# Output products by chunk with eight accumulating banks, half of the one-hots on ACT, and look-ups in half precision on DVE

## The chip, the core and the metric

The kernel runs on one core of a Trainium2 chip. The metric is the device time of one execution in microseconds (us), the median over runs. The core's engines work side by side, each through its own instructions in order: PE (matrix products; PEld is its weight load), DVE (vector), ACT (scalar functions, copies), POOL (general), SP (issues DMAs). They wait for each other by semaphores. PE writes into PSUM, eight banks of 128 x 512 f32 values; DVE and ACT empty them into SBUF.

## The reference

The model is a stack of blocks over 512 tokens of width 1024: a mixer of attentions, a mixture of experts (PEER), a gated projection, then two further blocks with their feed-forward parts. All is f32. The change lies in the PEER part alone:

```
s1, s2 = scores of the query's halves against 128 keys each
v1, i1 = top_k(s1, 16);  v2, i2 = top_k(s2, 16)
cand = v1[..., :, None] + v2[..., None, :]
sc, pos = top_k(cand, 16)
eidx = take_along_axis(i1 * 128 + i2, pos);  g = softmax(sc)
a = einsum('thkd,td->thk', expert_u[eidx], h)
out = einsum('thk,thkd->td', gelu(a) * g, expert_v[eidx])
```

There are 8 heads, 16 picks a head, so 128 picks a token, and 16384 experts.

## The kernel before

It computes PEER in two ways. For the first 128 tokens (`SP`) it fetches the picked rows by indirect DMA, 128 rows of u and then 128 of v for all tokens at once, and multiplies them on DVE (L1022, L1026; a "gather" below). For the other 384 (`ND`) it computes all experts: `up` takes the 128 chunks of 128 experts in turn, PE multiplies chunk and tokens, ACT applies Gelu out of the bank (L1088) and writes it to the DRAM array `ad`. Meanwhile a dense matrix G of weights is built in the DRAM array `Gd`: for each token the one-hots of i1 and i2 (L960, L961), the second one multiplied by the weight's upper and lower part (L964, r1 and r2), and a product of 128x128 per token and part on PE (L939), evacuated by ACT (L941) and written every 24 tokens (L945). In the down half, `ad` and G come back, DVE multiplies them (L1081), ACT rounds the product to its upper part (L113) and DVE takes the lower part (L1068).

Every f32 product with weights is three matmuls: upper weights by upper activations (L198), upper by lower (L199), lower by upper (L200). A unit of weights, 128 x 1024, is loaded by SP (L89) into one of four raw buffers, split by ACT into wh (four buffers) and by DVE into wl (L107, three buffers). `take` hands out unit i after it has issued wl of unit i+2, wh of i+3 and the load of i+6.

The down half before: 16 groups of eight chunks. `prepare(g + 1)` makes all of a group's activations while group g runs; PE begins a group when all eight are issued. For each of eight output blocks it makes 24 matmuls into one of two mm banks, and DVE adds the bank to x (L1122).

Side work is issued by generators. After every 12 counted matmuls `tick` steps them: `fetched` (gathers, one every `pace` ticks, in the down half spread over 228 ticks), `routing` (`select`, which picks experts for 128 tokens with the look-ups at L898, L901 and L905, and `build_g`, eight tokens a step), `prepare`, `load_g`. A chunk of 24 matmuls has two ticks, after its 6th matmul (tick A) and its 18th (tick B). A step of `build_g` takes 3 or 4 ticks by turns; its products (`g_products`) are issued one tick after r1 and r2, in two halves of four tokens.

In up the banks are the two mm banks; the products use s, the transposes pt.

Of the kernel before, what the change touches and what calls it, by code (L numbers as in the profile page):

```python
# [15 lines left out]
OP = mybir.AluOpType  # L16
# [17 lines left out]


class Net:
    def __init__(self, tc, ctx, a, units):
# [17 lines left out]
        self.width = T  # L55
# [691 lines left out]
    def peer(self, ctx):  # L747
# [8 lines left out]
        u_ctx = ExitStack()  # L756
        self.slots = u_ctx.enter_context(self.tc.tile_pool(name="slot2", bufs=19))
# [4 lines left out]
        io16, iota2 = fixed("io16", 16), fixed("iota2", 256, F16)  # L762
# [79 lines left out]
        def select(i):  # L842


            fi = slot("If")
# [40 lines left out]
            nc.vector.tensor_tensor(r[0], r[0], r[2], OP.add)  # L886
            nc.vector.tensor_tensor(r[1], r[1], r[3], OP.add)
# [5 lines left out]
            for half in range(2):  # L893
                tab = fi[:, half * 128:(half + 1) * 128].rearrange("p (h a) -> p h a", h=8)
                for hp in range(4):
                    e = slot("eq")
                    e3 = e.rearrange("p (s a) -> p s a", a=16)
                    nc.vector.tensor_tensor(e3, io16[:, None, :].to_broadcast([128, 32, 16]),  # L898
                                            r[half][:, hp * 32:hp * 32 + 32, None].to_broadcast([128, 32, 16]), OP.is_equal)
                    e4 = e.rearrange("p (h s a) -> p h s a", h=2, s=16)  # L900
                    nc.gpsimd.tensor_tensor(e4, e4, tab[:, 2 * hp:2 * hp + 2, None, :].to_broadcast([128, 2, 16, 16]), OP.mult)  # L901
# [24 lines left out]
            sel[i] = o  # L926
# [22 lines left out]
        def build_g(i):  # L949
            o = sel.pop(i)  # L950
            it = iota2.rearrange("p (i t) -> p i t", t=2)[:, None].to_broadcast([128, 4, 128, 2])
            for t in range(0, 128, 8):
# [10 lines left out]
                for j, r in enumerate((r1, r2)):  # L963
                    nc.vector.tensor_tensor(r, o2, col(2 + j), OP.mult)  # L964
# [3 lines left out]
        self.pace = 3  # L968

        def routing():  # L970
# [5 lines left out]
            for i in range(1, 4):  # L976
                nxt = select(i + 1) if i < 3 else None
                for n, w in enumerate(build_g(i)):
# [3 lines left out]
                    if i == 2 and nxt is None:  # L982
                        self.pace = 2
# [4 lines left out]
            self.pace = 1  # L988
            yield from load_g(0)
            yield 2  # L990
            self.spawn(prepare(0))
            yield from load_g(1)

        gather = {"tile": lambda: self.hp.tile([128, D], F32, tag="a", name=self.nm("row"))}
# [8 lines left out]
        def fetched():  # L1003
# [4 lines left out]
            def fetch(n):  # L1008
                if n < len(jobs):
                    m, k = jobs[n]  # L1010
                    rows[n] = gather["tile"]()
# [4 lines left out]
            for n, (m, k) in enumerate(jobs):  # L1016
                if self.pace is None and not left:
                    left.append(spread(len(jobs) - n, 228))
                yield next(left[0], 1) if left else self.pace
# [12 lines left out]
            for b in range(2):  # L1032
                yield 1
                pt = self.psum("pt")
                for j in range(4):
                    c = 4 * b + j
                    nc.tensor.transpose(pt[:, j * 128:(j + 1) * 128], y_tok[:, c * 128:(c + 1) * 128], self.ident)
                for j in range(4):
                    x = self.x[4 * b + j][:, 0:SP]
                    nc.vector.tensor_tensor(x, pt[:, j * 128:(j + 1) * 128], x, OP.add)  # L1040
            y_done.append(1)

        C, G, ready = {}, {}, {g: 0 for g in range(16)}
# [7 lines left out]
        def prepare(g):  # L1051

            if g:
                C[g] = [parts(self.act_tile()) for _ in range(8)]
            else:
                C[g] = [tuple(v[:, 0:ND] for v in p) for p in pairs(8, "C")]
            gt = G.pop(g)
            src = {}

            def fetch(k):  # L1060
                if k < 8:
                    src[k] = (self.hp.tile([128, D], F32, tag="a", name=self.nm("ar")) if g < 2 and k % 2 else self.slot("ar"))[:, 0:ND]
                    nc.sync.dma_start(src[k], ad[g * 8 + k])

            def split(k, a):
                self.round_hi(C[g][k][0], a)
                yield 1
                nc.vector.tensor_tensor(C[g][k][1], a, C[g][k][0].bitcast(F32), OP.subtract)  # L1068
                ready[g] += 1

            def split_later(k, a):
                yield 2
                yield from split(k, a)
            fetch(0)
            fetch(1)
            for k in range(8):
                fetch(k + 2)
                yield 1 + k % 2
                a = src.pop(k)
                v = a.rearrange("p (b t) -> p b t", t=TB)  # L1080
                nc.vector.tensor_tensor(v, v, gt[:, :, k * TB:(k + 1) * TB], OP.mult)  # L1081
                self.spawn(split_later(k, a))
# [11 lines left out]

        def up(c):
            self.width = ND
            self.linear(hh, 1, lambda _, ps: gelu(c, ps))
            self.width = T
# [9 lines left out]
        self.width = ND  # L1108
        self.pace = None
        for g in range(16):  # L1110
            last = g == 15
            until(lambda: ready[g] == 8)
            if g == 1:
                u_ctx.close()
                self.slots = ctx.enter_context(self.tc.tile_pool(name="slot3", bufs=7))
                rows = ctx.enter_context(self.tc.tile_pool(name="rows3", bufs=6))
                wide = lambda dt=F32: rows.tile([128, D], dt, tag="row", name=self.nm("row"))
                gather["tile"] = wide

            def evac(c, ps):  # L1120
                x = self.x[c][:, SP:]
                nc.vector.tensor_tensor(x, ps, x, OP.add)  # L1122
                if last:
                    if c == 0:
                        self.norm_begin(self.gains[:, 16:24])
                    self.norm_chunk(c)
            if not last:
                self.spawn(prepare(g + 1))
                if g < 14:
                    self.spawn(load_g(g + 2))  # L1130
            else:
                until(lambda: y_done)
                pp = []
                for k in range(2):
                    p = h_tok[:, k * 512:(k + 1) * 512]
                    nc.scalar.dma_start(p, self.a["p"][k])
                    t = wide(F32R)
                    pp.append((t[:, 0:512], t[:, 512:1024]))
                    self.hilo(p, *pp[k])
            for c in range(8):  # L1140
                self.linear_one(C[g], c, evac)
            C.pop(g)
        self.width = T
        t = [y_tok, h_tok, wide(), wide()]
        self.ple(pp, [v[:, k * 512:(k + 1) * 512] for v in t for k in range(2)])

    def linear_one(self, act, c, evac):
        self.linear(act, 1, lambda _, ps: evac(c, ps))
# [534 lines left out]
def host(i):  # L1683
# [44 lines left out]
    v = i["peer_expert_v"][0].reshape(128, 16, 8, 8, 128)  # L1728
    o["peer_v"] = v.transpose(1, 3, 0, 2, 4).reshape(128, 128, 1024)
# [66 lines left out]
```

## Time and profile before

| | us |
|---|---|
| median of 3 runs (2986.84 to 2990.61) | 2987.37 |
| the profiled execution | 2987.24 |
| its span, first to last instruction | 2985.5 |
| PE busy | 2877.2 (96%) |
| DVE busy | 1997.2 (67%) |
| ACT busy | 1255.2 (42%) |
| POOL busy | 558.8 (19%) |

The profile is of one execution. Busy PE time includes the pipelining of matmuls, so that two of them overlap in it. The PEER part lies from about 440 to 1762 us: queries, first selections and up chunks to 700, products beside up chunks to 1110, the last up chunks to 1195, the down half to 1762. [...]

### The profile page before, as it was taken

The page shows a single profiled execution, that of the slowest core. Times are in us where ns is not written, and L with a number is a line of the kernel's source. Part 1 is how long each engine was busy: PE and PEld are TensorE (multiplying, and loading weights), DVE is VectorE, ACT ScalarE, POOL GpSimd, SP SyncE. Part 2 cuts the span into 40 slices and gives each one's busy share as a digit, 9 for nine tenths or more (in the row PEclk, how much of TensorE's full clock was granted, in tenths as well). Part 3 has the DMA queues.
Part 4 walks back from the last instruction along what each step waited for, and adds up shares of the span by engine and source line. Part 5 has one row for each costly group of instructions (what it writes and reads, how often), then busy time and mean ns, then how long its engine had stood idle before and what let it go on. Part 6 is the DMA issues. An engine that isn't in the chain of part 4 may idle for free.

```text
span 2985.5 us, 40321 instructions
## 1 busy us (share of the span) xinstructions
PE 2877.2 (96%) x15329; PEld 2515.6 (84%) x15329; DVE 1997.2 (67%) x3593; ACT 1255.2 (42%) x1746; POOL 558.8 (19%) x512
## 2 busy tenths in 40 slices
PE   8999999998999999999999999999999989999998
PEld 6777787998999998899999997778888778888886
DVE  4565567699888768899999957754433585543442
ACT  5564533344666653333333354434222433442331
POOL 1020010023313225233333211120000240100001
PEclk9999999999999999999999999999999999999999
DMA  4321232357888999999999832223333211233331
GB/s 143 103 74 59 84 113 80 120 176 239 279 274 283 320 341 407 354 364 374 367 362 366 294 120 84 64 86 93 100 98 99 84 50 50 79 98 99 93 98 64
DMA packets 199713, 525.08 MB, mean 176 GB/s; under 512 B 19424, under 2 KB 86512, under 8 KB 199520
## 3 DMA queue, kind: packets, MB, share of 16 engines
q1 hardware_dynamic: 108144, 332.09, 33.0%
q0 software_dynamic: 37760, 136.28, 12.5%
q10 hardware_dynamic: 53616, 54.14, 5.4%
q8 instruction: 121, 1.98, 0.3%
q14 instruction: 72, 0.59, 0.1%
HBM read 470.00 MB, written 52.43 MB: 175 GB/s over the span
## 4 chain that ended last, share of the span: by engine, by line
PE 48%; DVE 13%; DMA 4%; issue 3%; ACT 1%; SPq 0%; ACTq 0%; POOL 0%; POOLq 0%; DVEq 0%
PE mm L198 14%; PE mm L199 14%; PE mm L200 14%; DMA ar<-ad 4%; DVE wl L107 4%; DVE y_tok L1026 3%; DVE a L1068 1%; DVE x L1122 1%; DVE ar L1081 1%; PE s L939 1%; DVE row L1022 1%; PE s L1504 1%; DMA raw<-in_peer_u_dram 0%; PE s L1250 0%; PE o L1539 0%
## 5 line engine op out<-in xcount | busy, mean ns | idle before, releaser
L198 PE MATMUL mm<-a,wh 128*128 128x384 f32 (+1 forms) x3832 | 1420.8, 371 | 32.7 <-DVE x L1122 15.1
L200 PE MATMUL mm<-a,wl 128*128 128x384 f32 (+1 forms) x3832 | 1393.9, 364 | 9.6 <-DVE wl L107 9.6
L199 PE MATMUL mm<-a,wh 128*128 128x384 f32 (+1 forms) x3832 | 1391.8, 363 | 0.6 <-DVE a L1240 0.6
L198 PEld LDWEIGHTS mm<-a,wh 128*128 128x128 f32 x3832 | 725.4, 189 | 131.4 <-ACT a L113 21.6
L200 PEld LDWEIGHTS mm<-a,wl 128*128 128x128 f32 x3832 | 724.5, 189 | 87.2 <-DVE wl L107 12.2
L199 PEld LDWEIGHTS mm<-a,wh 128*128 128x128 f32 x3832 | 725.6, 189 | 70.9 <-DVE a L1240 1.2
L113 ACT ACTIVATE wh<-raw 128x1024 fp32r<-128x1024 f32 x528 | 556.1, 1054 | 507.1 <-PE mm L199 347.5
L107 DVE TENSOR_TENSOR wl<-raw,wh 128x1024 fp32r<-128x1024 f32 x528 | 650.5, 1232 | 127.3 <-issue 54.8
L1012 POOL DMA_INDIRECT row<-in_rows_u_dram,at x128 | 162.9, 1272 | 322.9 <-DVE row L1022 268.7
L1012 POOL DMA_INDIRECT row<-in_rows_v_dram,at x128 | 158.9, 1241 | 269.2 <-DVE y_tok L1026 245.9
L261 POOL TENSOR_TENSOR ss<-ss,sq 128x512 f32<-128x512 f32 x42 | 65.2, 1553 | 630.2 <-ACT sq L260 630.2
L1026 DVE SCALAR_TENSOR_TENSOR y_tok<-row,w_tok,y_tok 128x1024 f32<-128x1024 f32 x127 | 162.6, 1280 | 0.2
L1022 DVE SCALAR_TENSOR_TENSOR row<-row,h_tok 128x1024 f32<-128x1024 f32 x128 | 161.5, 1266 | 0.4 <-DMA row<-in_rows_u_dram,at 0.4
L941 ACT ACTIVATE st<-s 128x512 f32<-128x512 f32 x96 | 136.8, 1445 | 48.8 <-PE s L939 46.3
L1344 DVE SCALAR_TENSOR_TENSOR t<-mm,rstd 128x512 f32<-128x512 f32 x62 | 42.9, 691 | 160.7 <-PE mm L200 160.7
L1356 DVE TENSOR_TENSOR x<-mm,x 128x512 f32<-128x512 f32 x48 | 33.2, 692 | 161.0 <-PE mm L200 161.0
L1345 ACT ACTIVATE t<-t 128x512 f32<-128x512 f32 x64 | 40.4, 632 | 199.4 <-DVE t L1344 199.4
L113 ACT ACTIVATE a<-ar 128x384 fp32r<-128x384 f32 x120 | 62.4, 524 | 146.0 <-DVE ar L1081 141.5
L1088 ACT ACTIVATE a<-mm 128x384 f32<-128x384 f32 x128 | 68.2, 532 | 117.9 <-PE mm L200 115.4
L1081 DVE TENSOR_TENSOR ar<-ar,G 128x384 f32<-128x384 f32 x128 | 70.7, 555 | 48.7 <-DMA ar<-ad 35.7
L901 POOL TENSOR_TENSOR eq<-eq,If 128x512 f32<-128x512 f32 x32 | 49.1, 1545 | 270.9 <-DVE eq L898 217.9
L200 PE MATMUL mm<-hid,wl 128*128 128x512 f32 x256 | 99.6, 389 | 0.0
(371 smaller groups left out, 2837.0 us busy)
## 6 DMA issues: line engine op xcount, KB each, us to landing
raw<-in_peer_u_dram SPq DMA_DIRECT2D x128, 512.0 KB
raw<-in_peer_v_dram SPq DMA_DIRECT2D x128, 512.0 KB
raw<-in_ffn_w_dram SPq DMA_DIRECT2D x128, 512.0 KB
ad<-a ACTq DMA_DIRECT2D x128, 192.0 KB
Gd<-st ACTq DMA_DIRECT2D x16, 1536.0 KB
G<-Gd SPq DMA_DIRECT2D x64, 384.0 KB
ar<-ad SPq DMA_DIRECT2D x128, 192.0 KB
raw<-in_w_in_dram SPq DMA_DIRECT2D x43, 512.0 KB
```

What stands on the lines that cost most here:

```text
L107: eng.tensor_tensor(l, r, h.bitcast(F32), OP.subtract)
L113: self.nc.scalar.activation(h, x, AF.Copy)
L198: self.nc.tensor.matmul(ps, w, ah, start=(k == 0), stop=False)
L199: self.nc.tensor.matmul(ps, w, al, start=False, stop=False)
L200: self.nc.tensor.matmul(ps, cols(wl, k), ah, start=False, stop=(k == K - 1))
L261: nc.gpsimd.tensor_tensor(self.ss, self.ss, sq, OP.add)
L941: nc.scalar.activation(st[:, :, t0 + 4 * b:t0 + 4 * b + 4].rearrange("p i t -> p t i"), pg.rearrange("p (t i) -> p t i", t=4), AF.Copy, sc ...
L1012: nc.gpsimd.indirect_dma_start(rows[n], None, self.a["rows_" + m], bass.IndirectOffsetOnAxis(ap=at[:, k:k + 1], axis=0))
L1022: nc.vector.scalar_tensor_tensor(r, r, 1.0, h_tok, OP.mult, OP.mult, accum_out=a_tok[:, k:k + 1])
L1026: nc.vector.scalar_tensor_tensor(y_tok, r, w_tok[:, k:k + 1], y_tok, OP.mult, OP.add)
L1081: nc.vector.tensor_tensor(v, v, gt[:, :, k * TB:(k + 1) * TB], OP.mult)
L1088: nc.scalar.activation(a, ps, AF.Gelu)
```

## The change

The down half goes chunk by chunk. Eight banks (all of PSUM) are kept open as accumulators, one for each output block, over all 128 chunks; a unit of weights is now one chunk's 128 experts by 1024 outputs. For the last eight chunks (`LAST`) the weights are laid out by output block again, so that the blocks end one after the other. The token-major result of the first 128 tokens is transposed by PE into the same banks, and DVE adds each bank to x once, 512 wide. `prepare` is one generator over chunks, three chunks ahead of what is used. The pools slot3 and rows3 are gone; gathered rows stay in hp. Gathers have other paces: 3 and 2 ticks by turns for 3, then 2, then 2 and 1 by turns for 1, then the rest spread over 236 ticks.

In up the chunks use the banks mm, o, mm by turns. In `build_g` r1 is made by ACT, token by token, with a scale from a tile; r2 stays on DVE. The evacuation at L941 iterates tokens innermost. In `select` the look-ups are f16, and the multiply at L901 moves from POOL to DVE.

```
-                ps = self.psum("o" if self.pend == [] else "mm")[:, 0:self.width]
+                ps = self.psum("o" if self.pend == [] else next(self.bank))[:, 0:self.width]
...
-        io16, iota2 = fixed("io16", 16), fixed("iota2", 256, F16)
+        io16, iota2 = fixed("io16", 16, F16), fixed("iota2", 256, F16)
-            fi = slot("If")
+            fi = slot("If").bitcast(F16)
+            rank = [fi[:, 256 + k * 128:384 + k * 128] for k in range(2)]
+            nc.vector.tensor_tensor(rank[0], r[0], r[2], OP.add)
+            nc.vector.tensor_tensor(rank[1], r[1], r[3], OP.add)
-                    e = slot("eq")
+                    e = slot("eq").bitcast(F16)[:, 0:512]
-                    nc.gpsimd.tensor_tensor(e4, e4, tab[:, 2 * hp:2 * hp + 2, None, :].to_broadcast([128, 2, 16, 16]), OP.mult)
+                    nc.vector.tensor_tensor(e4, e4, tab[:, 2 * hp:2 * hp + 2, None, :].to_broadcast([128, 2, 16, 16]), OP.mult)
...
-                nc.scalar.activation(st[:, :, t0 + 4 * b:t0 + 4 * b + 4].rearrange("p i t -> p t i"),
-                                     pg.rearrange("p (t i) -> p t i", t=4), AF.Copy, scale=2.0 ** -14)
+                nc.scalar.activation(st[:, :, t0 + 4 * b:t0 + 4 * b + 4],
+                                     pg.rearrange("p (t i) -> p i t", t=4), AF.Copy, scale=2.0 ** -14)
...
-                for j, r in enumerate((r1, r2)):
-                    nc.vector.tensor_tensor(r, o2, col(2 + j), OP.mult)
+                nc.vector.tensor_tensor(r2, o2, col(3), OP.mult)
+                for k in range(8):
+                    nc.scalar.activation(r1[:, k // 2, :, k % 2], o2[:, k // 2, :, k % 2], AF.Copy, scale=w[:, t + k:t + k + 1])
...
+        def prepare():
+            src = {}
+            def fetch(c):
+                if c < 128:
+                    src[c] = slot("ar")[:, 0:ND]
+                    nc.sync.dma_start(src[c], ad[c])
+            def split(c, a):
                 yield 2
+                C[c] = parts(self.act_tile())
+                self.round_hi(C[c][0], a)
+                yield 1
+                nc.vector.tensor_tensor(C[c][1], a, C[c][0].bitcast(F32), OP.subtract)
+                ready.add(c)
             fetch(0)
             fetch(1)
+            for c in range(128):
+                while c > len(used) + (3 if c < 120 - LAST else LAST + 1):
+                    yield 1
+                if c % 8 == 0 and c < 120:
+                    self.spawn(load_g(c // 8 + 1))
+                fetch(c + 2)
+                yield 2 if c < 120 - LAST else 1
+                a = src.pop(c)
                 v = a.rearrange("p (b t) -> p b t", t=TB)
+                nc.vector.tensor_tensor(v, v, G[c // 8][:, :, c % 8 * TB:(c % 8 + 1) * TB], OP.mult)
+                self.spawn(split(c, a))
...
+        one, outs = self.bank, itertools.cycle(("mm", "o", "mm"))
...
+        acc = [self.psum(t) for t in ("mm", "mm", "s", "s", "pt", "pt", "o", "n")]
+        def down(n, w, c, stop=False):
+            wh, wl = w
+            h, l = C[c]
+            o = acc[n][:, SP:]
+            nc.tensor.matmul(o, wh, h, start=(c == 0), stop=False, skip_group_check=True)
+            nc.tensor.matmul(o, wh, l, start=False, stop=False, skip_group_check=True)
+            nc.tensor.matmul(o, wl, h, start=False, stop=stop, skip_group_check=True)
+            self.counted()
+        for c in range(128 - LAST):
+            until(lambda: c in ready)
+            w = self.take()
+            for n in (2, 3, 4, 5, 6, 7, 0, 1):
+                down(n, cut(w, n), c)
+            C.pop(c)
+            used.append(c)
+        until(lambda: y_done and len(ready) == 128)
...
+        for n in range(8):
+            w = self.take()
+            nc.tensor.matmul(acc[n][:, 0:SP], y_tok[:, n * 128:(n + 1) * 128], self.ident, start=False, stop=False,
+                             is_transpose=True, skip_group_check=True)
+            for j in range(LAST):
+                down(n, cut(w, j), 128 - LAST + j, j == LAST - 1)
+            nc.vector.tensor_tensor(self.x[n], acc[n], self.x[n], OP.add)
```

## Rows read from the trace of the kernel before

**Rows 1.** Timeline of PE: start, duration (us), instruction. Plain stretch, then a step's products.
```profile
1402.38 0.33 PE L200 MATMUL mm<-a,wl 128*128 128x384 f32 x1
...
1402.90 0.33 PE L200 MATMUL mm<-a,wl 128*128 128x384 f32 x1
...
1002.43 0.24 PE L939 MATMUL s<-a 128*128 128x128 f16 x1
...
1002.88 0.42 PE L198 MATMUL mm<-a,wh 128*128 128x384 f32 x1
```
**Rows 2.** Windows: busy (x instructions) of PE, PEld, DVE, ACT, POOL; clock; DMA share, GB/s.
```profile
640.00:700.00 60.00, 49.49 (x247) 46.54 (x246) 59.73 (x144) 19.02 (x25) 30.42 (x21) 0.91 0.61 208
700.00:1110.00 410.00, 403.18 (x2777) 387.40 (x2777) 345.45 (x610) 260.87 (x275) 109.72 (x88) 1.00 0.87 293
1110.00:1195.00 85.00, 75.86 (x415) 74.28 (x414) 63.97 (x98) 29.83 (x43) 46.75 (x33) 0.96 1.04 407
1195.00:1762.00 567.00, 542.62 (x3060) 527.23 (x3058) 508.06 (x689) 205.02 (x266) 185.10 (x151) 1.00 0.91 337
```
**Rows 3.** Waits by stage (us, times, longest): selections, products, end of up, down.
```profile
PE mm L200 <- DVE wl L107: 9.6, 6, 4.6
...
PE s L939 <- DVE a L964: 6.9, 7, 2.9
...
PE mm L198 <- ACT a L1088: 9.1, 4, 5.0
...
DVE ar L1081 <- DMA ar<-ad: 26.5, 14, 3.8
...
PE mm L198 <- DVE x L1122: 19.5, 28, 2.3
```
**Rows 4.** Groups of DVE, 1197 to 1760 us: count | busy, mean ns | idle before.
```profile
L1026 DVE SCALAR_TENSOR_TENSOR y_tok<-row,w_tok,y_tok 128x1024 f32<-128x1024 f32 x127 | 162.6, 1280 | 0.2
...
L1122 DVE TENSOR_TENSOR x<-mm,x 128x384 f32<-128x384 f32 x128 | 70.7, 552 | 19.6 <-PE mm L200 19.6
...
L1022 DVE SCALAR_TENSOR_TENSOR row<-row,h_tok 128x1024 f32<-128x1024 f32 x23 | 28.1, 1220 | 0.0
```
**Rows 5.** Timeline of DVE, down half, without idle time between.
```profile
1400.23 1.22 DVE L107 TENSOR_TENSOR wl<-raw,wh 128x1024 fp32r<-128x1024 f32 x1
1401.36 1.28 DVE L1026 SCALAR_TENSOR_TENSOR y_tok<-row,w_tok,y_tok 128x1024 f32<-128x1024 f32 x1
```
**Rows 6.** DVE under POOL's multiply: timeline; then two lines' durations (min/median/max, ns).
```profile
632.28 1.16 DVE L898 TENSOR_TENSOR eq<-io,abf 128x512 f32<-128x512 f32 x1
...
940.21 2.00 DVE L1022 SCALAR_TENSOR_TENSOR row<-row,h_tok 128x1024 f32<-128x1024 f32 x1
...
L961 DVE TENSOR_TENSOR a<-iota,idxT 128x1024 f16<-128x1024 f16 x48 | 32.8, 684 | 0.0
...
L898 DVE TENSOR_TENSOR eq<-io,abf x32: 677/684/1793, 628.6 to 939.0; 128x512 f32<-128x512 f32 x32
```
**Rows 7.** Lines' durations, min/median/max in ns.
```profile
L889 ACT ACTIVATE sp<-sp,rtok x4: 402/402/403, 628.1 to 891.2; 128x128 f32<-128x128 f32 x4
...
L941 ACT ACTIVATE st<-s x96: 1420/1438/1567, 701.2 to 1106.9; 128x512 f32<-128x512 f32 x96
...
L348 ACT ACTIVATE t<-mm x35: 575/1107/1214, 31.6 to 2506.6; 128x512 f32<-128x512 f32 x35
...
L687 DVE TENSOR_TENSOR w<-w,pt x2: 680/684/689, 315.2 to 354.8; 128x512 f32<-128x512 f32 x2
```
**Rows 8.** Timelines of DVE and ACT around two steps of the products.
```profile
1000.71 1.29 DVE L964 TENSOR_TENSOR a<-a,idxT 128x1024 f16<-128x1024 f16 x2
...
999.57 0.61 ACT L1088 ACTIVATE a<-mm 128x384 f32<-128x384 f32 x1
...
1000.64 1.06 ACT L113 ACTIVATE wh<-raw 128x1024 fp32r<-128x1024 f32 x1 [0.46 <-ACT a L1088]
...
1009.45 2.31 ACTq L1089 DMA_DIRECT2D ad<-a  x1
```

More of the change, by code (lines that the diff above doesn't have):

```diff
@@ L33 @@
 LEAD = 6
+LAST = 8
 class Net:
@@ L54, in __init__ @@
         self.n_mm = 6
-        self.width = T
+        self.width, self.bank = T, itertools.cycle(["mm"])
         self.mm_done, self.timed, self.pend = 0, [], None
@@ L755, in peer @@
         dram = ctx.enter_context(self.tc.tile_pool(name="dram2", bufs=1, space=bass.MemoryType.DRAM))
-        u_ctx = ExitStack()
-        self.slots = u_ctx.enter_context(self.tc.tile_pool(name="slot2", bufs=19))
+        self.slots = ctx.enter_context(self.tc.tile_pool(name="slot2", bufs=19))
         slot, pairs = self.slot, self.pairs
@@ L987, in routing @@
             yield 3
-            self.pace = 1
+            self.pace = itertools.cycle((2, 1))
             yield from load_g(0)
             yield 2
-            self.spawn(prepare(0))
-            yield from load_g(1)
-        gather = {"tile": lambda: self.hp.tile([128, D], F32, tag="a", name=self.nm("row"))}
+            self.spawn(prepare())
         y_done = []
@@ L1010, in fetch @@
                     m, k = jobs[n]
-                    rows[n] = gather["tile"]()
+                    rows[n] = self.hp.tile([128, D], F32, tag="a", name=self.nm("row"))
                     nc.gpsimd.indirect_dma_start(rows[n], None, self.a["rows_" + m],
@@ L1017, in fetched @@
                 if self.pace is None and not left:
-                    left.append(spread(len(jobs) - n, 228))
-                yield next(left[0], 1) if left else self.pace
+                    left.append(spread(len(jobs) - n, 2 * (128 - LAST) - 4))
+                yield next(left[0], 1) if left else next(self.pace)
                 r = rows.pop(n)
@@ L1031, in fetched @@
                     nc.vector.tensor_tensor(w_tok[:, b], w_tok[:, b], a_tok[:, b], OP.mult)
[L1032 to L1040, printed above, removed]
             y_done.append(1)
-        C, G, ready = {}, {}, {g: 0 for g in range(16)}
+        C, G, ready, used = {}, {}, set(), []
         def load_g(g):
@@ L1093, in until @@
                 self.tick()
+        one, outs = self.bank, itertools.cycle(("mm", "o", "mm"))
         def up(c):
-            self.width = ND
+            self.width, self.bank = ND, outs
             self.linear(hh, 1, lambda _, ps: gelu(c, ps))
-            self.width = T
+            self.width, self.bank = T, one
         self.norm_start(lambda: self.spawn(true_h()))
@@ L1107, in peer @@
             up(c)
-        self.width = ND
         self.pace = None
[L1110 to L1148, printed above, removed]
+        acc = [self.psum(t) for t in ("mm", "mm", "s", "s", "pt", "pt", "o", "n")]
[7 more added lines that the diff above has]
+            self.counted()
@@ new lines, in peer @@
+        cut = lambda w, n: tuple(v[:, n * 128:(n + 1) * 128] for v in w)
+        for c in range(128 - LAST):
[6 more added lines that the diff above has]
+        until(lambda: y_done and len(ready) == 128)
+        pp = []
+        for k in range(2):
+            p = slot("p")
+            nc.scalar.dma_start(p, self.a["p"][k])
+            pp.extend(pairs(1, "pp"))
+            self.hilo(p, *pp[k])
@@ new lines, in peer @@
+        for n in range(8):
[5 more added lines that the diff above has]
+            nc.vector.tensor_tensor(self.x[n], acc[n], self.x[n], OP.add)
+            if n == 0:
+                self.norm_begin(self.gains[:, 16:24])
+            self.norm_chunk(n)
@@ L1150, in peer_units @@
+        C.clear()
+        self.ple(pp, [slot("pw") for _ in range(8)])
     def peer_units(self):
```

42 lines of the change are left out of this document (10 added, 32 removed).

## The prediction

> **What bounds the kernel now.** First the page: PE is busy 96% of the span, the next engine, DVE, 67%. A busy PE can still be held up, so I count starts in the timeline. In an undisturbed stretch three matmuls of 128x384 start in 0.52 us, 0.173 us each; a step's half of eight f16 products starts in 0.45, 0.057 each [rows 1]. A chunk of 24 is 4.16 us. The windows by stage give instruction counts [rows 2]; count times interval against length is what PE loses:
> - 640 to 700 (first selections): 243 x 0.173 + 0.4 = 42.5 of 60; lost 17.5.
> - 700 to 1110 (one-hot products): 2003 x 0.173 + 768 x 0.057 + 0.7 = 391.7 of 410; lost 18.3.
> - 1110 to 1195 (end of the up half): 415 x 0.173 = 71.9 of 85; lost 13.1.
> - 1195 to 1762 (the down half): 3040 x 0.173 + 12 x 0.227 + 0.9 = 530.5 of 567; lost 36.5.
>
> These 85 us are all the change can win; every other stage keeps its code. What ends each loss is in the waits by stage [rows 3]: x at L1122 in the down half, a at L1088 (the Gelu that empties a bank) at the end of up, wl in the selections, the one-hots at L964 in the products. DVE is busy 90% of the down half and over 99% of the first selections [rows 2]; a wait on it is a late DVE.
>
> **Down half, output blocks in eight banks.** PE does the same 3072 matmuls, and the transposes move. Gone: 128 adds at L1122 of 0.55 us [rows 4]. PE's 28 waits for them show 19.5 us [rows 3]; a wait is counted from the modelled end of the last matmul, 0.33 - 0.17 us after the next could have started, so 28 x 0.16 more: 24. Of the 12.5 that the windows lose beyond them I put a third, 4, to the other waits at the start of a group and of the transposes, which go too: 28 in all.
>
> What is late next: the lower half of a chunk's activations. Before, a whole group of eight stood ready. Now, by the code, tick A of chunk i issues the G product of chunk i+2 and the rounding of i+1, tick B the subtraction for i+1, and PE's second matmul of i+1 wants it. DVE can't start a chunk early: wl of i+2 takes the buffer that PE's last matmul of i-1 frees, seen 0.3 us after the chunk's start (a matmul's 0.33 us less its interval, and the signal). From there by start-to-start times: wl 1.13 and gather 1.20 (the second's own 1.28 less the same 0.09 of overlap) [rows 5], G product 0.46 and subtraction 0.55 to its end, both of L1122's shape and put at its price [rows 4]: 3.64, against the 4.33 at which PE wants it. With two gathers in a chunk it is 4.84: late by 0.51, with the signal 0.58. 151 gathers lie in the down half (L1022 and L1026, and the first of v at L1024) [rows 4]; the new paces leave as many (2.5 ticks for 3 until the selections end: 46 done for 38; then 35 as now; then 24 for 36, so 105 done of 256). Spread over 236 ticks they have 2 x 151 - 236 = 66 gaps of one tick, half inside one chunk: 33 x 0.58 = 19 us. Gain 28 - 19 = **9 us**. Bounds: 28 if the doubles hide; below nothing if loads are late (rival 2).
>
> The loads of ar are now issued 6 ticks (12.5 us) ahead for 4.5, and without a group's burst of three plus G; DVE waited for them 14 times, 26.5 us in all [rows 3], and I count no wait for PE from it. The other edits of this half (rows in hp, slots kept, x added 512 wide for 384 + 128) have nothing waiting for them: DVE's load falls by 70.7 us.
>
> **End of up, third bank.** Four waits for Gelu, 9.1 us, longest 5.0 [rows 3], and a granted clock of 0.96 [rows 2]. ACT, in order, comes late to them, while its queue holds ad issues, wh and the a_tok that waits for the last gather of u. With mm, o, mm a chunk may be emptied one chunk (4.16 us) later: only about 1 us of the longest is left. The waits cost 9.8 with the supplement; gain 8.8, and half of the 3.3 us that the windows lose beyond them, by the clock: **10.5 us** (bounds 5, if wl becomes late instead, and 13).
>
> **Selections, POOL's multiply on DVE.** While POOL multiplies, DVE's two-input instructions stretch: eq from 0.68 to as much as 1.79, a gather from 1.22 to 2.00 [rows 6]. Eight eq, nine gathers and ten wl are stretched so, 27 from 632.3 to 940.2 us (the first and the last in rows 6), by some 0.75 us in the mean: an estimated 21 us of DVE time, which goes. In its place DVE gets 32 multiplies. Two-input f16 of 1024 elements takes 0.68, as f32 of 512 does [rows 6]: f16 runs two for one, so 512 should take 0.34 to 0.42, next start 0.1 earlier: 32 x 0.33 = 10.6 us (bound 0.60: 19). I leave eq and the reduction at 0.68. DVE sheds 10 of 21 us. PE lost 17.5 us in 640 to 700 (clock 0.91), 9.6 of it seen as waits for wl, and 6.9 in the products [rows 2, 3], nearly all under these multiplies; half goes: **12 us** (bounds 2 and 20).
>
> [...]
>
> **Products, half of the one-hots on ACT.** DVE loses 48 x 0.60 us (r1 and r2 together 1.29) [rows 8]; ACT gains 48 x 8 copies of 128x128 with a scale from a tile. The nearest row is L889, 0.402 [rows 7]; if neighbours on ACT overlap by 0.1, as on DVE [rows 5], 0.30 each: four in 1.3, eight in 2.5 us (bounds 0.30 and 0.40). Against it stands the evacuation L941, 1.44 us, which writes every element 96 bytes from the last; now it writes runs of four and reads PSUM with 512 bytes between neighbours. Bounds: 0.58 (the shortest of L348, contiguous) and 1.44. DVE reads PSUM at that distance at L687 in 0.684, no longer than the eq of as many f32 from SBUF [rows 6, 7]: I take 0.60.
>
> Where the one-hots fall: a step takes 3 or 4 ticks by turns, so two of four are issued at tick A with products at tick B of the same chunk. Today they are ready 0.44 us ahead there (DVE ends at 1002.0, PE starts at 1002.43) [rows 1, 8]. On ACT the chunk begins with Gelu (999.57), the ad issue and wh (1000.64 to 1001.70), so r1 starts at 1001.6; the first four end at 1002.9, signal 0.06: PE waits 0.5. 24 x 0.5 = 12 us. After each Gd issue the next ad issue takes about 2 us, as at 1009.45 [rows 8]; Gd comes every third step, and one in four falls before a tick A: 4 x 1.9 = 7.6. The steps at tick B have 2.5 to 3 us. Cost **20 us**.
>
> Does ACT keep up? In 14 ticks, 7 chunks and 4 steps, PE needs 7 x 4.16 + 4 x 0.91 = 32.8 us. ACT: 7 x 2.03 (Gelu to the end of wh, less the overlap) + 32 x 0.30 + 8 x (p - 0.1) + 1.33 x 2 = 26.4 + 8 (p - 0.1), p the evacuation's price: 30.4 at 0.60, even with PE at p = 0.9. So it does, barely.
>
> **The sum.** 9 + 10.5 + 12 - 20 = 11.5 us off the profiled execution's 2987.24 (span 2985.5): 2976. The median of the runs shown is 2987.37, so nothing is to be shifted.
>
> **Rivals.**
> 1. ACT becomes the bound of the products (slower). If the evacuation keeps a strided price, 1.11 (the upper of L348's two sizes) to 1.44, ACT needs 34.5 to 37.1 us for 32.8 [rows 7]. That is 1.7 to 4.3 a round, 12 rounds: 20 to 52 us, above the waits, since ACT is then never ahead. Time 2996 to 3028, decided at p = 0.9; copies at 0.40 instead of 0.30 do the same (3.2 a round). For it: L941 is the dearest write in the trace. Against: L687.
> [...]
> 2. DMA takes the down half's gain. Its engines are busy 0.91 at 337 GB/s over the stage, which makes 370 when full, but 407 was reached just before [rows 2]. A chunk at 4.16 us wants 512 + 192 + 192 + 1.28 x 512 KB, 380 GB/s. If 366 is the limit, 118 chunks take 491 x (380/366) = 510 us: 19 more; no gain, 2985 to 2995. DVE's waits for ar [rows 3] speak for it, the bursts behind them against.
> 3. The new waits don't come: ACT and DVE run ahead where I hold them back. Then 20 + 19 fall away: 2937; half of it, 2957.
> 4. The f16 multiply is no faster than f32 (0.60): selections win 2 for 12: 2986.
>
> **How the numbers follow.** Forecast 0.40 (2966 to 2986), rival 1 0.18, rival 2 0.14, rival 3 0.22 (2937 to 2965), rival 4 0.06. Faster by over 0.2%, below 2981: 0.22 + 0.31 of the forecast = 0.53. Within 0.2%, 6 us, about what a measurement can tell from no change: 0.09, half of rival 2 and rival 4 = 0.22. Slower: 0.18 + 0.07 = 0.25. Range 2945 to 3006: it leaves out the ends of rivals 1 and 3.
>
> **What would show it.** L1122 gone and DVE's a-subtraction releasing PE about 33 times for 0.5 us in the down half; L941 at 0.6; waits of PE's products on ACT, two in four steps; no wl above 1.3 us in the selections; Gelu waits at the end of up below 2 us. Wrong if L941 stays above 0.9, if PE waits for ar's DMA through DVE all along the down half, or if the products lose over 30 us.

## The result, and the profile after

The changed kernel takes 2956.64 us (median of 4 runs, 2951.12 to 2961.54) against 2987.73 for the kernel before: ratio 0.9887, 95% interval 0.9874 to 0.9900, so 31 us or 1.1% faster. The prediction was 2976, range 2945 to 3006: the sign and the range hold, the size is 2.7 times the forecast. The profiled execution took 2955.55 us, its span is 2953.8.

The windows by stage of the changed kernel, with the columns of [rows 2] (the clock is the profile's granted clock of TensorE, 1.00 being full speed) and bounds moved so that each holds about the same work:

```profile
640.00:695.00 55.00, 47.28 (x245) 44.72 (x244) 54.38 (x155) 20.04 (x29) 13.57 (x11) 0.94 0.72 246
695.00:1101.00 406.00, 401.86 (x2771) 385.34 (x2771) 323.27 (x594) 292.66 (x655) 84.00 (x77) 1.00 0.89 302
1101.00:1168.00 67.00, 67.00 (x389) 67.00 (x388) 46.82 (x67) 25.95 (x37) 24.57 (x19) 1.00 1.04 402
1168.00:1728.00 560.00, 546.71 (x3091) 535.47 (x3090) 464.25 (x576) 198.39 (x272) 263.11 (x158) 1.00 0.94 348
```

Counted as before (239, 1996, 387 and 3071 matmuls of 128x384 at 0.1733, the 768 products at 0.057, and the few others), PE now loses 13.2, 15.6, 0 and 24.6 us in the four stages, for 17.5, 18.3, 13.1 and 36.5. That is 4.3 + 2.7 + 13.1 + 11.9 = 32.0 us won, and the spans differ by 31.7. So the whole gain lies in these stages, and the account by starts finds all of it. PE's waits, in the order selections (first two), products (three), down half; at the end of up it has none. In the changed kernel's lines L109 makes wl, L115 wh, L202 is the third matmul of a plain product, L1109 to L1111 are the three of the down half, L943 is the one-hot products, L967 r2, L969 the copies for r1 and L1079 Gelu:

```profile
PE mm L202 <- DVE wl L109: 5.1, 4, 2.2
PE o L202 <- DVE wl L109: 2.1, 2, 1.5
...
PE s L943 <- DVE a L967: 1.6, 3, 0.6
PE s L943 <- ACT a L969: 1.2, 2, 0.8
PE s L943 <- DVE eq L900: 1.0, 1, 1.0
...
PE s L1110 <- DVE a L1059: 13.3, 33, 2.8
```

Set beside [rows 3]: the 28 waits for x are gone, 33 for the lower half of the activations (a at L1059) stand in their place, the four for Gelu have gone without a successor, and the products wait for ACT twice. The durations that the prediction had to guess (min/median/max in ns; L903 is the look-ups' multiply, L900 its comparison, L945 the evacuation, L969 a copy for r1):

```profile
L903 DVE TENSOR_TENSOR eq<-eq,If x32: 424/425/428, 629.1 to 930.9; 128x512 f16<-128x512 f16 x32
L900 DVE TENSOR_TENSOR eq<-io,If x32: 680/685/690, 628.3 to 930.2; 128x512 f16<-128x512 f16 x32
L945 ACT ACTIVATE st<-s x96: 569/580/601, 696.2 to 1098.7; 128x512 f32<-128x512 f32 x96
L969 ACT ACTIVATE a<-a,idxT x384: 419/426/437, 693.9 to 1096.1; 128x128 f16<-128x128 f16 x192
```

All four are where the prediction put them or within 0.02 us of it (0.34 to 0.42, 0.68, 0.60; a copy starts 0.29 after the last, for 0.30). What was wrong is therefore not a price of one instruction but who waits for what, and when.

### The profile page after: what moved, and what is told of

Read it like the earlier page. It is cut to its first block, busy times and chain, and to the rows that moved or that the text cites. A ratio compares the mean times of both kernels' runs of the same rounds, so it can differ in the third digit from the quotient of the medians.

```text
span 2953.8 us, 40425 instructions
## 1 busy us (share of the span) xinstructions
PE 2868.0 (97%) x15329; PEld 2511.1 (85%) x15329; DVE 1910.8 (65%) x3452; ACT 1278.2 (43%) x2130; POOL 563.2 (19%) x480
## 4 chain that ended last, share of the span: by engine, by line
PE 57%; DVE 5%; issue 2%; DMA 1%; ACT 1%; POOL 0%; POOLq 0%; DVEq 0%; SPq 0%; ACTq 0%
PE mm L200 13%; PE mm L201 12%; PE mm L202 12%; DVE y_tok L1029 2%; PE s L1110 1%; PE s L1111 1%; PE pt L1109 1%; PE pt L1110 1%; PE pt L1111 1%; PE mm L1111 1%; PE mm L1109 1%; PE mm L1110 1%; PE s L1109 1%; PE o L200 1%; PE o L201 1%
## 5 line engine op out<-in xcount | busy, mean ns | idle before, releaser
L200 PE MATMUL mm<-a,wh 128*128 128x512 f32 (+1 forms) x2528 | 974.8, 386 | 5.2 <-ACT t L350 3.7
L202 PE MATMUL mm<-a,wl 128*128 128x512 f32 (+1 forms) x2528 | 953.9, 377 | 5.1 <-DVE wl L109 5.1
L201 PE MATMUL mm<-a,wh 128*128 128x512 f32 (+1 forms) x2528 | 952.7, 377 | 3.3 <-DVE a L140 2.7
L115 ACT ACTIVATE wh<-raw 128x1024 fp32r<-128x1024 f32 x528 | 556.2, 1054 | 637.8 <-issue 256.0
L109 DVE TENSOR_TENSOR wl<-raw,wh 128x1024 fp32r<-128x1024 f32 x528 | 643.8, 1220 | 226.0 <-PE mm L1111 70.7
L200 PEld LDWEIGHTS mm<-a,wh 128*128 128x128 f32 x2528 | 478.4, 189 | 89.7 <-issue 12.4
L202 PEld LDWEIGHTS mm<-a,wl 128*128 128x128 f32 x2528 | 477.7, 189 | 81.6 <-DVE wl L109 6.4
L201 PEld LDWEIGHTS mm<-a,wh 128*128 128x128 f32 x2528 | 478.5, 189 | 73.4 <-DVE a L140 3.1
L1015 POOL DMA_INDIRECT row<-in_rows_u_dram,at x128 | 150.5, 1176 | 623.1 <-DVE row L1025 348.4
L1015 POOL DMA_INDIRECT row<-in_rows_v_dram,at x128 | 224.9, 1757 | 219.8 <-PE mm L1111 173.5
L200 PE MATMUL o<-a,wh 128*128 128x384 f32 (+1 forms) x384 | 134.9, 351 | 7.8 <-ACT wh L115 7.8
L202 PE MATMUL o<-a,wl 128*128 128x384 f32 (+1 forms) x384 | 132.1, 344 | 2.1 <-DVE wl L109 2.1
L201 PE MATMUL o<-a,wh 128*128 128x384 f32 (+1 forms) x384 | 131.7, 343 | 1.6 <-DVE a L249 1.6
L969 ACT ACTIVATE a<-a,idxT 128x128 f16<-128x128 f16 x384 | 118.8, 426 | 0.0
L1110 PE MATMUL s<-a,wh 128*128 128x384 f32 x256 | 89.3, 349 | 13.3 <-DVE a L1059 13.3
L202 PE MATMUL mm<-hid,wl 128*128 128x512 f32 x256 | 99.6, 389 | 0.0
```

Source lines behind the costliest of these rows:

```text
L109: eng.tensor_tensor(l, r, h.bitcast(F32), OP.subtract)
L115: self.nc.scalar.activation(h, x, AF.Copy)
L200: self.nc.tensor.matmul(ps, w, ah, start=(k == 0), stop=False)
L201: self.nc.tensor.matmul(ps, w, al, start=False, stop=False)
L202: self.nc.tensor.matmul(ps, cols(wl, k), ah, start=False, stop=(k == K - 1))
L969: nc.scalar.activation(r1[:, k // 2, :, k % 2], o2[:, k // 2, :, k % 2], AF.Copy, scale=w[:, t + k:t + k + 1])
```

## The experiments

Medians of one kernel vary: the kernel before lies between 2987.7 and 2993.2 us. So beside the median stands its ratio to the kernel before as measured with it, and where the trace of one execution puts the difference: three stretches between starts of PE's 128x384 matmuls, by their number, which every kernel here has in the same count. A stretch that an edit doesn't reach differs by up to 4 us between two traces; smaller differences are not read as effects. 0 to 2688 holds the selections and products; 2688 to 3456 the end of up and the first 16 chunks (in the kernel before two groups) of the down half; 3456 to 6143 the rest of it.

| kernel | median us | ratio to before, interval | 0-2688 | 2688-3456 | 3456-6143 |
|---|---|---|---|---|---|
| before | 2987.7 to 2993.2 | | 612.4 | 155.7 | 494.0 |
| changed | 2956.6 | 0.9887 (0.9874 to 0.9900) | 604.9 | 135.9 | 488.3 |
| r1_on_dve | 2954.5 | 0.9885 (0.9870 to 0.9901) | 604.5 | 135.2 | 486.7 |
| evac_strided | 2968.1 | 0.9922 (0.9908 to 0.9936) | 618.9 | 136.7 | 488.0 |
| copies_backwards | 2963.1 | 0.9910 (0.9896 to 0.9924) | 610.3 | 135.7 | 488.3 |
| pool_multiply | 2959.4 | 0.9905 (0.9891 to 0.9920) | 611.2 | 136.4 | 486.4 |
| f32_multiply | 2964.8 | 0.9913 (0.9898 to 0.9928) | 613.9 | 136.9 | 486.1 |
| one_bank_kind | 2959.6 | 0.9900 (0.9885 to 0.9916) | 606.7 | 138.6 | 489.8 |
| bank_alone | 2989.1 | 0.9999 (0.9989 to 1.0009) | 612.5 | 155.3 | 494.6 |
| pace_alone | 2990.1 | 0.9998 (0.9988 to 1.0007) | 615.4 | 144.4 | 503.5 |
| denser_gathers | 2964.9 | 0.9912 (0.9898 to 0.9926) | 607.8 | 141.2 | 492.6 |
| lead_four | 2932.9 | 0.9812 (0.9799 to 0.9826) | 604.7 | 133.1 | 470.5 |
| lead_four_dense_end | 2945.2 | 0.9847 (0.9830 to 0.9864) | 604.8 | 148.4 | 466.7 |
| lead_four_gd_on_sp | 2927.5 | 0.9781 (0.9767 to 0.9796) | 600.5 | 133.1 | 466.7 |

**Half of the one-hots on ACT.** Three kernels, from the changed one. r1_on_dve takes the copies back:

```
-                nc.vector.tensor_tensor(r2, o2, col(3), OP.mult)
-                for k in range(8):
-                    nc.scalar.activation(r1[:, k // 2, :, k % 2], o2[:, k // 2, :, k % 2], AF.Copy, scale=w[:, t + k:t + k + 1])
+                for j, r in enumerate((r1, r2)):
+                    nc.vector.tensor_tensor(r, o2, col(2 + j), OP.mult)
```

> The changed kernel with r1 made by DVE again, as before; the contiguous evacuation and all else stay. Theory (the copies on ACT cost PE only what its products wait for them, about 5 us in the changed kernel, and DVE has room for 0.60 us a step): 2949 to 2957, and the waits of the products are again on DVE. Rival (taking 29 us from DVE in the products stage is itself a gain, because wl and the look-ups come earlier): slower than the changed kernel's 2956.6 by 5 to 15 us, 2962 to 2972, with waits for wl in the products stage.

The intervals lie over each other and the stretches agree within 2 us, as the theory has it: the move costs nothing that can be measured and wins nothing. PE's waits in the products are 6.7 us for DVE (8 times, the old r1 and r2) in place of the 3.8 of the changed kernel. The rival is out.

copies_backwards keeps them on ACT in another order:

```
-                for k in range(8):
+                for k in (3, 2, 1, 0, 7, 6, 5, 4):
```

> The changed kernel with ACT's eight copies of r1 in the order 3, 2, 1, 0, 7, 6, 5, 4, so that the first product needs the fourth copy. Theory (r1 on ACT is cheap only because the products take the copies in the order in which they come, one token at a time; for the whole of four PE would wait): the fourth copy ends 0.23 us after the first product's start and is seen 0.06 later: 24 x 0.29 = 7 us more, 2961 to 2966, with waits of the products on ACT in every second step. Rival (ACT is ahead of PE anyway): no change, 2954 to 2959.

By the median 6.5 us slower (the two intervals overlap by a little), by the stretch 5.4. The timelines of one step show why. The changed kernel, ACT then PE (start, duration):

```profile
990.44 0.49 ACT L1079 ACTIVATE a<-o 128x384 f32<-128x384 f32 x1 [0.49 <-PE o L202]
...
991.34 1.06 ACT L115 ACTIVATE wh<-raw 128x1024 fp32r<-128x1024 f32 x1 [0.40 <-ACT a L1079]
992.30 2.48 ACT L969 ACTIVATE a<-a,idxT 128x128 f16<-128x128 f16 x8
...
993.19 0.34 PE L202 MATMUL mm<-a,wl 128*128 128x384 f32 x1
993.37 0.24 PE L943 MATMUL s<-a 128*128 128x128 f16 x1
```

The first copy ends at 992.73 and the fourth at about 993.6, after the products have begun at 993.37; yet no product waits, since the fourth token is wanted only 0.37 us into them, at 993.74. With the copies backwards the first product is late, by 0.29:

```profile
997.16 0.34 PE L202 MATMUL mm<-a,wl 128*128 128x384 f32 x1
997.33 0.10 PEld L943 LDWEIGHTS <-a 128*128 128x128 f16 x1 [0.16 <-issue]
...
997.62 0.22 PE L943 MATMUL s<-a 128*128 128x128 f16 x1
```

Such a gap of 0.285 to 0.29 us stands there 18 times, 5.2 us, where the changed kernel has 0.01. So PE takes the copies token by token, and in the order in which they are wanted they cost it nothing.

evac_strided puts the evacuation's loop order back:

```
-                nc.scalar.activation(st[:, :, t0 + 4 * b:t0 + 4 * b + 4],
-                                     pg.rearrange("p (t i) -> p i t", t=4), AF.Copy, scale=2.0 ** -14)
+                nc.scalar.activation(st[:, :, t0 + 4 * b:t0 + 4 * b + 4].rearrange("p i t -> p t i"),
+                                     pg.rearrange("p (t i) -> p t i", t=4), AF.Copy, scale=2.0 ** -14)
```

> The changed kernel with the evacuation of the products as before, tokens outermost (1.44 us for 0.58), r1 still on ACT. Theory (the copies fit on ACT only because the evacuation shrank): ACT then needs 7 x 1.87 + 32 x 0.30 + 8 x 1.34 + 2.1 = 35.5 us in a round in which PE needs 32.8, so 2.7 us x 12 rounds = 32 us slower than the changed kernel: 2980 to 2995, PE waiting on ACT all along the products. Rival (PE takes the copies one token at a time and ACT's lateness stays hidden): 2956 to 2966.

11.5 us slower, 14 by the stretch: more than the rival allows and under half of the theory's 32. The evacuation takes 1.43 again (last row below), and ACT's own waits for PE between 700 and 1100 us fall from 61.4 us to 9.1. The changed kernel first, then evac_strided:

```profile
ACT st L945 <- PE s L943: 28.4, 20, 1.7
ACT a L1079 <- PE mm L202: 23.5, 22, 2.3
...
ACT a L1079 <- PE o L202: 9.5, 11, 2.3
```

```profile
ACT a L1079 <- PE mm L202: 6.2, 7, 1.7
ACT st L945 <- PE s L943: 2.9, 6, 0.8
...
L945 ACT ACTIVATE st<-s x96: 1417/1428/1570, 698.8 to 1116.1; 128x512 f32<-128x512 f32 x96
```

So ACT did become the bound, as the first rival of the prediction has it. The size was off on both sides: from the first to the last product the stage takes 417.3 us, 34.8 a round and not 35.5, and the changed kernel 403.2, 33.6 a round and not PE's bare 32.8.

**The look-ups.** pool_multiply moves the f16 multiply back:

```
-                    nc.vector.tensor_tensor(e4, e4, tab[:, 2 * hp:2 * hp + 2, None, :].to_broadcast([128, 2, 16, 16]), OP.mult)
+                    nc.gpsimd.tensor_tensor(e4, e4, tab[:, 2 * hp:2 * hp + 2, None, :].to_broadcast([128, 2, 16, 16]), OP.mult)
```

> The changed kernel with the look-ups' multiply on POOL again, in f16. Theory (POOL's multiply stretches DVE's two-input instructions beside it, as in the kernel before, whatever the type): wl of up to 2 us in the selections, waits for wl longer than the changed kernel's 7.2, 5 to 12 us slower than it: 2961 to 2969. Rival (the gain of the selections came from half the data; in f16 POOL is short and disturbs little): 2952 to 2959, no wl above 1.5 us.

By the median 2.8 us slower, within both intervals and at the edge of the rival, so the times don't decide; by the stretch 6.3. The stretching is in the trace: with the multiply on POOL, where it takes 1.17 us in f16 for the 1.30 in f32 of the kernel before, wl stretches to 2.60 (first row) and the comparison to 1.67, where in the changed kernel no wl exceeds 1.24 (second row) and no comparison 0.69. Why the two engines disturb each other is not shown.

```profile
L109 DVE TENSOR_TENSOR wl<-raw,wh x72: 1203/1226/2602, 602.7 to 957.2; 128x1024 fp32r<-128x1024 f32 x72
```

```profile
L109 DVE TENSOR_TENSOR wl<-raw,wh x74: 1196/1224/1239, 599.1 to 957.0; 128x1024 fp32r<-128x1024 f32 x74
```

f32_multiply keeps DVE and takes away half precision:

```
-        io16, iota2 = fixed("io16", 16, F16), fixed("iota2", 256, F16)
+        io16, iota2 = fixed("io16", 16), fixed("iota2", 256, F16)
-            fi = slot("If").bitcast(F16)
+            fi = slot("If")
-                    e = slot("eq").bitcast(F16)[:, 0:512]
+                    e = slot("eq")
```

> The changed kernel with the look-ups on DVE, but in f32 (tables, comparison, multiply and reduction). Theory (DVE's time in the selections is what counts; the f32 multiply takes about 0.68 for 0.425): 32 x 0.26 = 8 us more of DVE, half of it seen by PE: 3 to 6 us slower than the changed kernel, 2958 to 2963, waits for wl of 9 to 13 us up to 700. Rival (it is enough that POOL no longer multiplies): 2954 to 2958, waits for wl as in the changed kernel, 7.2.

8.2 us slower, 9.0 by the stretch, more than the theory's 3 to 6. The multiply takes 0.692 us for 0.425:

```profile
L903 DVE TENSOR_TENSOR eq<-eq,If x32: 691/692/695, 629.9 to 937.2; 128x512 f32<-128x512 f32 x32
```

That is 32 x 0.27 = 8.5 us more of DVE. Waits for wl up to 695 us are 11.2 for 7.2, and the products wait 8.7 us for 3.8. By PE's starts the difference falls in two parts. Up to 930 us it is 4.6, half of DVE's time as the theory has it: 3.5 around the first selections, where DVE is busy 99% of the time, the rest in the products. The other 4.6 come at once at 940 to 949 us, where ACT's ad issue behind a Gd store takes 5.91 us for 1.55 at the same place of the changed kernel, PE waits 2.4 us for r1, and the granted clock is 0.86 (from 938 to 950). What the multiply has to do with that issue is not shown.

So from the changed kernel the multiply back on POOL costs some 6 us of its first stretch and f32 some 4.5, not counting that issue. These two don't add up to what the look-ups win over the kernel before: no kernel here has both undone.

**The end of up.** one_bank_kind leaves only the third bank out:

```
-        one, outs = self.bank, itertools.cycle(("mm", "o", "mm"))
+        one, outs = self.bank, itertools.cycle(("mm",))
```

> The changed kernel with the up chunks in the two mm banks alone, as before. Theory (the third bank is what removed the waits for Gelu at the end of up): 2967 to 2971, four or so waits for Gelu of 9 to 13 us in all between 1100 and 1185 us, and a granted clock below 1.00 there. Rival (the waits went because the gathers of u end elsewhere with the new paces, and ACT has no late a_tok there): 2956 to 2959, no waits.

The theory falls: 3.0 us by the median, 2.7 by the stretch, no more than stretches differ by, and one wait for Gelu, after an ad issue of 8.3 us:

```profile
PE mm L200 <- ACT a L1079: 2.1, 1, 2.1
```

The other three stay away without the bank. bank_alone is the counterpart, the kernel before with only this edit (and the argument that carries the bank):

```
-                ps = self.psum("o" if self.pend == [] else "mm")[:, 0:self.width]
+                ps = self.psum("o" if self.pend == [] else next(self.bank))[:, 0:self.width]
```

> The kernel before with one part of the change alone: up chunks use the banks mm, o, mm by turns. The prediction's term for it was 10.5 us. Theory (in the kernel before the bank does cover the four waits for Gelu, since each is shorter than or near a chunk; in the changed kernel the new order of prepare and the new paces cover most of them as well, so that undoing the bank there cost only 3 us): 7 to 11 us under the kernel before, with at most one wait for Gelu left at the end of up, of about 1 us. Rival (three of the four waits come from DVE's backlog, and a bank only moves them): at most 3 us under it, waits for Gelu of 5 us or more left.

Nothing: 0.9999, and 155.3 us for 155.7 in the stretch. The waits for Gelu are indeed gone, but they only change their name. At the end of up PE now waits for wl, and in the down half the longest wait for x grows from 2.3 [rows 3] to 5.7:

```profile
PE mm L200 <- DVE wl L107: 2.8, 2, 2.4
PE o L200 <- DVE wl L107: 2.4, 1, 2.4
...
PE mm L198 <- DVE x L1124: 24.9, 28, 5.7
```

So the bank only changes what PE waits for, and the waits that are left are for DVE. pace_alone therefore lightens DVE there, in the kernel before: gathers every 2 and 1 ticks for one every tick.

```
-            self.pace = 1
+            self.pace = itertools.cycle((2, 1))
...
-                yield next(left[0], 1) if left else self.pace
+                pace = self.pace if isinstance(self.pace, int) or left else next(self.pace)
+                yield next(left[0], 1) if left else pace
```

> The kernel before with one part of the change alone: at the end of up a gather every 2 and 1 ticks by turns for one every tick; the down half then has some 12 gathers more. Theory (DVE's backlog from the gathers there made three of the four waits for Gelu, and the first waits of the down half): from the start of the 2688th to that of the 3456th matmul of 128x384 it takes 8 to 16 us less than the kernel before's 155.7, with one wait for Gelu of about 2.4 us left; the down half gives part of it back, as 12 gathers are 14 us more of DVE: 4 to 12 us under the kernel before in all. Rival (prepare of eight chunks, not the gathers, makes the backlog): at most 4 us less in that stretch, and no gain in all.

Half right. From the 2688th to the 3072nd matmul DVE has 21 gathers to do for 31. The stretch takes 11.3 us less, with one wait for Gelu left, the one behind the long ad issue. But the down half, now with 162 gathers for 152, gives 9.5 of it back, and there is no gain in all (the 3.0 in the first stretch, which the edit doesn't touch, is this one run's). Its waits for x are 26.5 us for 19.5:

```profile
PE mm L198 <- ACT a L1089: 3.2, 1, 3.2
...
PE mm L198 <- DVE x L1123: 26.5, 32, 2.4
```

lead_four_dense_end is the same test from the other end, in the kernel of the next part:

```
-            self.pace = itertools.cycle((2, 1))
+            self.pace = itertools.cycle((1,))
```

> lead_four (2932.9) with the gathers at the end of up one every tick, as in the kernel before, for 2 and 1 by turns. Theory (at the end of up DVE was behind, with a gather every tick beside the first activations; the new pace takes that load off, and not the bank): waits for Gelu or wl come back at the end of up, 4 to 12 us more there, 2935 to 2945. Rival (the new prepare, which makes four chunks ahead of the down half for eight, is what took DVE's load off): no waits at the end of up, 2930 to 2935.

12.3 us slower than lead_four, 15.3 in the stretch (3.8 come back later), with waits for wl of up to 2.2 us. So it is the gathers' pace that relieves the end of up. Why the changed kernel keeps the gain and pace_alone does not can be read from the counts: of the ten gathers that leave the end of up, the changed kernel does eight before it (81 up to the 2688th matmul for 73, by the pace of 3 and 2), and its down half has 154, nearly as many as before, and 70.7 us of adds less. Which of the two keeps the gain is not shown: no kernel here has one without the other. Nor is it told apart where the other 7.3 us come from by which lead_four_dense_end's stretch is shorter than that of the kernel before.

**The down half.** Does PE wait for the second gather of a chunk? denser_gathers:

```
-                    left.append(spread(len(jobs) - n, 2 * (128 - LAST) - 4))
+                    left.append(spread(len(jobs) - n, 200))
```

> The changed kernel with the down half's gathers spread over 200 ticks for 236. Theory (PE waits for the subtraction once in every chunk with two gathers): 2 x 151 - 200 = 102 gaps of one tick, half of them inside a chunk, so 51 waits for 33, 18 x 0.57 = 10 us more: 2965 to 2969; none in the last 36 ticks. Rival (the waits follow something else in the chunk, such as the load of G or ar): as many as before, 2955 to 2959.

8.3 us slower by the median, 9.6 over the two last stretches, with 47 waits for a at L1059 for 33 (51 were expected): the theory holds, the rival doesn't.

```profile
PE s L1110 <- DVE a L1059: 16.4, 47, 2.0
```

lead_four lets the activations be made one chunk earlier:

```
-                while c > len(used) + (3 if c < 120 - LAST else LAST + 1):
+                while c > len(used) + (4 if c < 120 - LAST else LAST + 1):
```

> The changed kernel with prepare four chunks ahead of what is used for three, so that a chunk's lower half is issued one chunk earlier. Theory (the 33 waits of PE for the subtraction, 18.7 us, are only due to where it stands in DVE's order in a chunk with two gathers): the waits go, 2938 to 2944. Rival (the DMA engines, at 0.94 busy and 348 GB/s, set the down half's pace): the waits move to raw, wl or ar, 2950 to 2957.

23.7 us faster than the changed kernel, more than the theory's 13 to 19, its interval clear of the other. One wait of 2.0 us is left of the 33. The two last stretches give 20.6: the 18.7 of the 33 waits, and part of 3.6 us by which the matmul after each wait came late too. The DMA engines carry it: 362 GB/s at 0.96 over the shorter stage, for 348 at 0.94 in the changed kernel.

```profile
PE s L1110 <- DVE a L1059: 2.0, 1, 2.0
...
1169.00:1706.00 537.00, 535.04 (x3081) 534.43 (x3080) 460.40 (x570) 197.20 (x269) 205.57 (x158) 1.00 0.96 362
```

lead_four_gd_on_sp adds one edit:

```
-                nc.scalar.dma_start(Gd[:, :, block, :].rearrange("g p n -> p g n"), st.rearrange("p (g i) t -> p g (i t)", g=16))
+                nc.sync.dma_start(Gd[:, :, block, :].rearrange("g p n -> p g n"), st.rearrange("p (g i) t -> p g (i t)", g=16))
```

> lead_four with the stores of Gd issued by SP for ACT. Theory (ACT's issue of ad after a Gd store takes 1.5 to 8 us because both go through ACT's queue; PE's long waits for r1, four of about 1 us, come from it): the ad issues after a Gd store fall to 0.33, PE's waits on ACT in the products under 1 us in all, the end of up unchanged; 3 to 6 us faster, 2926 to 2930. Rival (the store then holds up the weights' loads on SP's queue by as much): raw or wl late, 2933 to 2945.

5.4 us faster than lead_four. In the products, which the edit touches, the stretch is 4.2 shorter and no wait of PE for ACT is left. The last stretch is 3.8 shorter too, though the edit doesn't reach it; one wait of 2.0 us less is all that the trace shows for it. The ad issue after a Gd store took up to 7.90 us in lead_four (first row) and never over 0.36 here; SP's own weight loads beside it are issued in 0.33 us in the median, 2.60 at most (0.33 at most in lead_four):

```profile
L1080 ACTq DMA_DIRECT2D ad<-a x128: 325/326/7897, 510.2 to 1169.6; - x128
```

```profile
L1080 ACTq DMA_DIRECT2D ad<-a x128: 326/326/361, 510.8 to 1166.0; - x128
L91 SPq DMA_DIRECT2D raw<-in_peer_u_dram x128: 327/328/2600, 456.1 to 1142.4; - x128
```

This version beats both kernels: ratio 0.9781 to the kernel before.

## Why the prediction was right, and where its sizes were wrong

**Down half, forecast 9 us, found 11.9.** The mechanism is the one forecast, to the number: 33 waits for the lower half of the activations, 18.7 us by PE's starts for 19, and the waits for x gone. One of the 33, DVE then PE:

```profile
1370.73 1.28 DVE L1029 SCALAR_TENSOR_TENSOR y_tok<-row,w_tok,y_tok 128x1024 f32<-128x1024 f32 x1
1371.93 0.55 DVE L1059 TENSOR_TENSOR a<-ar,a 128x384 fp32r<-128x384 f32 x1
...
1372.53 0.44 PE L1110 MATMUL s<-a,wh 128*128 128x384 f32 x1 [0.31 <-DVE a L1059]
```

The second gather of the chunk stands ahead of the subtraction, which ends at 1372.48. Rival 2, the DMA engines, fell with lead_four. Beside these waits 30.6 us were won for the forecast 28. That the banks won them is read from the 28 waits for x that went; no kernel here has the eight banks alone.

**Selections, forecast 12, and one-hots on ACT, forecast -20: together -8, found +7.0.** The prices of the look-ups held (0.425 for 0.34 to 0.42, the comparison unchanged at 0.685). r1_on_dve tells the two terms apart: it has no copies on ACT, and its first stretch is 604.5 us, 7.9 below the kernel before and 0.4 below the changed one. So the selections won about 8 of the forecast 12 (what the shorter evacuation and the eight gathers that now come earlier add to it or take from it is not shown), and the copies cost nothing that can be measured, for 20.

What failed is the step "the first four end at 1002.9, signal 0.06: PE waits 0.5. 24 x 0.5 = 12 us". The signal of 0.06 is what the trace shows: in the kernel before a wl ends at 663.85 and PE starts on it at 663.91. The consumer was wrong: it let PE wait for all four copies, while each pair of products needs one; the wait is 0.01 us, and the waits on ACT in "two in four steps" are two in all. Its times were off too: the copies start 1.06 us before the products can, not 0.83, so the fourth ends 0.24 after that and not 0.47. copies_backwards, where the first product does need the fourth copy, has 0.29 there and not 0.5. The second part of that step, 4 x 1.9 behind the Gd issues, held in part: the ad issues behind Gd took 1.5 us or more in 9 of 16 cases, the last 8, but PE lost time to r1 behind three of them only, 4.3 us in all and not 7.6. Against that stand the waits for r1 on DVE that went: 6.7 us in r1_on_dve for r1 and r2, 1.6 for r2 alone now.

Rival 3, given 0.22, had just this for ACT: half of it, 2957. That the time falls on this very number is luck in part: the selections' 4 us too few are made up by the other two terms.

**End of up, forecast 10.5, found 13.1; the reason was wrong.** The step "with mm, o, mm a chunk may be emptied one chunk later: only about 1 us of the longest is left" does take the waits for Gelu away and is beside the point. bank_alone shows it worth 0, one_bank_kind no more than 3. The prediction had the new paces in hand ("24 for 36") and counted them only to find how many gathers are left for the down half (151, as before; the traces have 154 for 152), not as fewer at the end of up (21 for 31); pace_alone puts that at 11.3 us where it falls, given back later in the kernel before. That the right size came out is luck.

**Rival 1** was decided as the prediction said, by the evacuation's price: 0.58, far below 0.9, with ACT reading 512 bytes apart; evac_strided shows what the old price costs, 11.5 us and not the 20 to 52 of the rival. A read 512 bytes apart didn't make it dear: with it, and with writes in runs of 16 bytes, the evacuation takes 0.58; with a read in order and each f32 written 96 bytes from the last it takes 1.43. The edit changes read and write together, and no run changes one alone.

**Rival 4** fell with the 0.425. The multiply takes 0.425 in f16 for 0.692 in f32_multiply, while the comparison, whose second input repeats one element, takes 0.685 in both kernels; why half the data shortens the one and not the other is not shown.

## What to carry to other kernels

When an engine in the middle is behind, take work off it before you give its consumers more room: here a buffer there only moved the wait to the next name, and a lighter load at one place paid only where the load didn't come back at another. Where a consumer takes a producer's output piece by piece, compare piece with piece: here the order of the pieces was worth some 5 us, and which of the two engines made them nothing. Try a just-in-time step one round earlier: here that single number was worth 23.7 us, beside 31 for the whole change.

## What the runs showed of the hardware that was not expected

A multiply of 128x512 on POOL takes 1.17 us in f16 (pool_multiply) and 1.30 in f32 (the kernel before), where DVE takes 0.425 (the changed kernel) and 0.69 (f32_multiply). A DMA that ACT issues within 3 us of issuing the 1.5 MB store of Gd holds its sequencer for 1.5 to 8.4 us in 14 of the 16 cases in the kernel before and the changed one; with that store on SP's queue (lead_four_gd_on_sp) it takes 0.36 at most. An evacuation on ACT that reads PSUM 512 bytes apart and writes runs of four f32 takes 0.58 (the changed kernel), one that reads in order and writes each f32 96 bytes from the last 1.43 (evac_strided).
